# Memory tokens of row tiles 4 to 7 turned on VectorE instead of TensorE, their turns dealt out one by one, and the last sums in banks of their own

## The chip, the core and the metric

The kernel runs on one core of a Trainium2 chip. Its engines work side by side: TensorE (PE in the profile, with its weight loads as a row of their own, PEld), VectorE (DVE), ScalarE (ACT), GpSimd (POOL) and the sync engine (SP), whose queue issues most DMAs. The metric is the device time of one execution in microseconds (us), the median of several.

## What is computed

The reference is a trunk of two layers on 256 tokens of 2048 features, with 256 memory tokens beside them. Cut to what matters here:

```python
for l in range(DEPTH):                      # DEPTH = 2
    h = rmsnorm(x, norm_g[l])
    proj = h @ w_in[l]                      # 2048 -> 7168 columns, three groups of heads
    ...                                     # gated conv, differential attention
    mn = rmsnorm(mem, mem_norm_g[l])
    mkv = mn @ w_mem_kv[l]                  # 2048 -> 1024 columns: keys, values
    ...                                     # attention into the memory tokens
    y = jnp.concatenate([y_a, y_d, y_m], axis=-1) @ w_out[l]
    x = x + y
```

All inputs and the output are float32.

## The kernel before

**Splitting.** Every large product is made of three TensorE passes: each operand is split into a high part (rounded by ScalarE) and a low part (the remainder, taken by VectorE), and hi x hi, lo x hi and hi x lo are summed in PSUM (`products`, L310 to L312, for the input and output projections; the second `products`, L777, for the memory projection).

**The memory stage.** The first 95 us of the program project the memory tokens to keys and values of both layers. The contraction over 2048 features is cut into 16 row tiles of 128; g counts row tiles over both layers, 0 to 31 (`NG`). For every g one tile of weights, 128 rows by 1024 columns (512 KB), is loaded by `weights(g)` into one of four `raw` buffers, and `w_parts(g)` makes its parts: ScalarE multiplies by the norm's gain and rounds (L742), VectorE takes the remainder (L743). Gains of row tiles below `DEALT` come from `cva`, the others from `gm_dealt`. The tokens of row tile k must stand with features on the partitions. `token_parts(k)` splits them into `memT` (L261 on ScalarE, L262 on VectorE), and where they come from depends on `DEALT`, which is 8: below it, `turned(k)` has TensorE transpose two 128x128 blocks of `xs` against an identity (L748). From 8 on, a quarter of the tokens (four row tiles, 512 features) is read by `strips_of` in four DMAs of 128 KB, each to 32 partitions in runs of 512 bytes, and turned by one VectorE transpose of 128x1024 (`strips_turned`, L638); row k of a quarter is then feature 4p + j on partition p. The tokens in natural order are loaded as well for all 16 row tiles (`tokens`), since their squares are summed on ScalarE (`mem_squares`).

**The order.** The stage is written out by hand: `pin` keeps instructions in the order of the program on their engine. Twelve matmuls of 128x512 belong to each g: for each half of the columns two hi x hi (FIRST), then two lo-token x hi-weight and two hi-token x lo-weight (REST), for two halves of tokens. The loop over g (L885) issues FIRST of g, then `operands(g + 2)` (for g = 3 those of 4 and 5), then REST of g, then `beside(g)`, then the second half. `beside(g)` issues on SP's queue, in this order: the natural tokens that `TOKENS` has for g, `weights(g + 4)`, which waits until `w_parts(g)` has freed the buffer, and one small load of constants; then it appends tasks (strips, squares, statistics) that `run_side` carries on, a step for each g. SP issues in order, and the DMA engines serve what it issued in about that order.

Before the loop, SP issues tokens and weights of g = 0 to 3 in the order of L846 to L858, and `operands` of 1 to 3 are made in between.

**The strips of x.** In the same stage the four quarters of x are read as strips and turned (`x_turned`): strips, a pause, one transpose of 128x1024, then two row tiles split in each of two steps. `x_next` uses the same function between the layers.

**The tail.** The last output block (512 columns, second layer) is computed by `block` with `apart=4`: the products of the second half of the tokens (t = 1) for its last four row tiles are left to the end (`late`). Two of them run at full width; the last two run first for columns 0 to 255, then for columns 256 to 511, all in the one PSUM bank `acc[1]`. Then VectorE adds each half to `xs` (L1065) and the halves are stored by DMAs, the first issued by SP, the second by ScalarE's queue (L1068).

Of the kernel before, what the change touches and what calls it, by code (L numbers as in the profile page):

```python
# [11 lines left out]
F32 = mybir.dt.float32  # L12
# [3 lines left out]
ALU = mybir.AluOpType  # L16
# [3 lines left out]
P = 128  # L20
# [19 lines left out]
QT = NB // P  # L40
DEALT = 8

# [7 lines left out]
def encoder(ctx: ExitStack, tc: tile.TileContext, x, mem, norm_g, w_in, conv_w, conv_b,  # L50
# [242 lines left out]
    def block(stat, w, cols, order, steps=1, apart=0, acc=None, more=False,  # L293
# [8 lines left out]
        def ends(k):  # L302
            return k == order[0] and not begun, k == order[-1] and not more
# [14 lines left out]
        for c in range(0, n, CK):  # L318
# [11 lines left out]
            run_side(steps)  # L330
        for t, k, hi, lo in late[:-2]:
            products(acc, t, k, hi, lo, *ends(k))
        for at in range(0, NB, NB // 2):
            half = slice(at, at + NB // 2)
            for t, k, hi, lo in late[-2:]:
                products([a[:, half] for a in acc], t, k, hi[:, half], lo[:, half], False, at > 0 and ends(k)[1])
        return acc

# [296 lines left out]

    def strips_turned(st):
        whole = tmp.tile([P, QT, SEQ], F32, tag="sh", name=nm("xf"))
        pin(nc.vector.transpose(whole.rearrange("p j (n i) -> p j n i", i=B),  # L638
                                st.rearrange("p n (c j) -> p j n c", j=QT)))
        return whole  # L640

    def x_turned(dst, l, q, src, at_once):


        st = yield from strips_of(src, at_once)
        yield 2
        whole = strips_turned(st)
        yield
        for j in range(QT):
            split_T(dst, q * QT + j, whole[:, j], g_norm(l, q * QT + j), pin=True)  # L650
            if j % 2:
                yield

# [96 lines left out]

    dealt = {}

    def mem_turned(q, at_once):
        st = yield from strips_of(mem[:, q * NB:(q + 1) * NB], at_once)
        yield 2
        dealt[q] = strips_turned(st)

# [3 lines left out]

    def operands(g):
        token_parts(g)
        w_parts(g)

# [33 lines left out]

    TOKENS = {0: 4, 1: 6, 8: 8, 9: 10, 10: 12, 11: 14}  # L800
    MEM_STRIPS = {2: 2, 4: 3}
    X_STRIPS = {12: 0, 16: 1, 20: 2, 24: 3}
# [3 lines left out]
    def beside(g):  # L806


        if g + 4 < NG:
            if g in TOKENS:  # L810
                tokens(TOKENS[g], 2)
            weights(g + 4)
        if g in MEM_STRIPS:
            tasks.append(later(mem_turned(MEM_STRIPS[g], 2 if g == 2 else 1), 1))
        if g >= 2:
            for dst, src in islice(constants, 1):
                pin(nc.sync.dma_start(dst, src))
        if g in X_STRIPS:
            q = X_STRIPS[g]
            tasks.append(later(x_turned(xT, 0, q, x[:, q * NB:(q + 1) * NB], 1), 1))  # L820
        if g in (4, 8, 11, 13):
            mem_squares((4, 8, 11, 13).index(g))
        if g == 6:
            distance(1)
        if g == 13:
            tasks.append(later(mem_stats(), 1))
        if g == 21:
            tasks.append(later(rest_of_constants(), 1))
        if g in X_NATURAL:
            x_natural(*X_NATURAL[g])  # L830
        if g in X_SQUARES:
            for t in range(NT):
                x_square(X_SQUARES[g], t)
# [23 lines left out]
    tokens(3, 1)  # L857
    weights(3)  # L858
    warm(6)
    distance(0)  # L860
# [46 lines left out]
    for l in range(DEPTH):  # L907
# [149 lines left out]
        for b in range(4):  # L1057
# [3 lines left out]
            for t in range(NT):  # L1061
                n = 256 if final else NB
                for lo in range(0, NB, n):
                    xc = xs[:, t, b * NB + lo:b * NB + lo + n]
                    nc.vector.tensor_tensor(xc, acc[t][:, lo:lo + n], xc, ALU.add)  # L1065
                    if final:
# [37 lines left out]
```

## Time and profile before

| | us |
|---|---|
| median of 3 runs | 920.17 (920.02 to 920.51) |
| the profiled execution | 919.96 |
| its span, first to last instruction | 918.1 |
| TensorE busy | 913.5 |
| VectorE busy | 675.5 |
| ScalarE busy | 501.9 |
| granted TensorE clock | 0.999 of full |

The span is 1.86 us shorter than the time of the same execution. The profile gives for each engine its busy time, groups of instructions by source line, a timeline of instructions (start, length, engine, line, operation, what it writes and reads, shape, count of merged instructions, and in brackets idle time before it with what ended it), and the transfers of the DMA engines. A letter q behind an engine is its sequencer, which issues DMAs. Lengths of TensorE's records overlap, since matmuls are pipelined; what one costs is the distance from its start to the start of the next.

### The profile page before, as it was taken

The numbers are of one execution on the slowest core, as the hardware profiler recorded it, in microseconds if no ns is written. First come the engines' busy times: TensorE is split into PE (matmuls) and PEld (weight loads), VectorE is DVE, ScalarE is ACT, GpSimd is POOL, SyncE is SP. The second block draws the span as 40 slices with busy tenths as digits, with TensorE's granted clock in tenths as the row PEclk, the third lists the DMA queues.
The fourth block names the chain that finished last, engine by engine and source line by source line (L and its number), as shares of the span: only waits on it lengthen the run. The fifth ranks groups of instructions, "written<-read, shape, count | busy, mean of one in ns | idle before, by whom it ended". The sixth has DMA issues, their size and how long they took to land.

```text
span 918.1 us, 12328 instructions
## 1 busy us (share of the span) xinstructions
PE 913.5 (99%) x4183; PEld 759.4 (83%) x4183; DVE 675.5 (74%) x1197; ACT 501.9 (55%) x770; POOL 7.0 (1%) x18
## 2 busy tenths in 40 slices
PE   9999999999999999999999999999999999999998
PEld 7888888888888888888888888888888888888886
DVE  5889978767898777558676757878898777458652
ACT  6666745675545554446455544568555554446431
POOL 0001000000000000000000000000000000000000
PEclk9999999999999999999999999999999999999999
DMA  9999887875669997989677767885888887978662
GB/s 276 290 286 296 285 256 234 247 215 186 178 221 251 245 258 230 246 259 262 225 256 247 237 199 215 237 232 188 235 231 223 253 234 219 268 243 247 215 220 73
DMA packets 254243, 216.12 MB, mean 235 GB/s; under 512 B 131982, under 2 KB 181476, under 8 KB 254180
## 3 DMA queue, kind: packets, MB, share of 16 engines
q1 hardware_dynamic: 252020, 211.78, 78.4%
q0 software_dynamic: 672, 2.10, 0.7%
q10 hardware_dynamic: 1488, 1.46, 0.5%
q8 instruction: 33, 0.54, 0.2%
q14 instruction: 30, 0.25, 0.1%
HBM read 194.32 MB, written 20.97 MB: 234 GB/s over the span
## 4 chain that ended last, share of the span: by engine, by line
PE 99%; DVE 0%; DVEq 0%; issue 0%
PE acc L310 28%; PE acc L311 28%; PE acc L312 28%; PE acc L777 10%; PE po L447 2%; PE s L555 1%; PE s L554 1%; PE s L607 1%; PE warm L125 0%; PE pt L748 0%; DVE xs L1065 0%; DVEq L1099 0%; PE pva L862 0%; PE pvb L150 0%
## 5 line engine op out<-in xcount | busy, mean ns | idle before, releaser
L290 DVE TENSOR_TENSOR lo<-raw,hi 128x1024 fp32r<-128x1024 f32 x288 | 351.6, 1222 | 179.7 <-ACT hi L289 170.5
L289 ACT CAST hi<-raw 128x1024 fp32r<-128x1024 f32 x288 | 302.5, 1052 | 325.5 <-PE acc L312 254.7
L311 PE MATMUL acc<-lo,xT 128*128 128x512 f32 x896 | 349.0, 390 | 0.0
L312 PE MATMUL acc<-hi,xT 128*128 128x512 f32 x896 | 348.7, 389 | 0.0
L310 PE MATMUL acc<-hi,xT 128*128 128x512 f32 x896 | 348.4, 391 | 0.0
L312 PEld LDWEIGHTS acc<-hi,xT 128*128 128x128 f32 x896 | 168.2, 188 | 35.0
L310 PEld LDWEIGHTS acc<-hi,xT 128*128 128x128 f32 x896 | 168.2, 188 | 33.8
L311 PEld LDWEIGHTS acc<-lo,xT 128*128 128x128 f32 x896 | 168.3, 188 | 33.5
L311 PE MATMUL acc<-lo,yT 128*128 128x512 f32 (+1 forms) x258 | 99.9, 387 | 0.0
L312 PE MATMUL acc<-hi,yT 128*128 128x512 f32 (+1 forms) x258 | 99.9, 387 | 0.0
L310 PE MATMUL acc<-hi,yT 128*128 128x512 f32 (+1 forms) x258 | 99.9, 387 | 0.0
L777 PE MATMUL acc<-hi,memT 128*128 128x512 f32 (+1 forms) x260 | 70.6, 390 | 0.0
L310 PEld LDWEIGHTS acc<-hi,yT 128*128 128x128 f32 x258 | 48.4, 188 | 10.0
L312 PEld LDWEIGHTS acc<-hi,yT 128*128 128x128 f32 x258 | 48.4, 188 | 10.0
L311 PEld LDWEIGHTS acc<-lo,yT 128*128 128x128 f32 x258 | 48.4, 188 | 9.8
L777 PEld LDWEIGHTS acc<-hi,memT 128*128 128x128 f32 x260 | 47.9, 188 | 10.1 <-ACT hi L742 0.5
L777 PE MATMUL acc<-lo,memT 128*128 128x512 f32 (+1 forms) x130 | 39.7, 387 | 0.0
L777 PEld LDWEIGHTS acc<-lo,memT 128*128 128x128 f32 x130 | 24.3, 188 | 5.0
L743 DVE SCALAR_TENSOR_TENSOR lo<-raw,cva,hi 128x1024 fp32r<-128x1024 f32 (+2 forms) x21 | 21.4, 1027 | 6.4 <-ACT hi L742 6.3
L565 ACT ACTIVATE e<-e,mx 128x256 f32<-128x256 f32 x48 | 23.8, 498 | 1.4 <-DVE mx L561 1.3
L743 DVE SCALAR_TENSOR_TENSOR lo<-raw,gm_dealt,hi 128x1024 fp32r<-128x1024 f32 x16 | 20.5, 1279 | 4.7 <-ACT hi L742 3.8
L742 ACT ACTIVATE hi<-raw,cva 128x1024 fp32r<-128x1024 f32 (+2 forms) x21 | 19.7, 947 | 5.6 <-DMA raw<-in_w_mem_kv_dram 5.1
(155 smaller groups left out, 635.3 us busy)
## 6 DMA issues: line engine op xcount, KB each, us to landing
raw<-in_w_in_dram SPq DMA_DIRECT2D x192, 512.0 KB, 4.3
raw<-in_w_out_dram SPq DMA_DIRECT2D x64, 512.0 KB, 4.8
raw<-in_w_in_dram SPq DMA_DIRECT2D x64, 256.0 KB, 4.3
raw<-in_w_mem_kv_dram SPq DMA_DIRECT2D x29, 512.0 KB, 6.3
d<-sh SPq DMA_DIRECT2D x80, 128.0 KB, 3.8
sh<-d SPq DMA_DIRECT2D x64, 128.0 KB, 3.7
d<-yn SPq DMA_DIRECT2D x40, 64.0 KB, 4.5
yn<-d SPq DMA_DIRECT2D x40, 64.0 KB, 3.0
```

The source lines that it names most:

```text
L289: nc.scalar.copy(hi, raw)
L290: nc.vector.tensor_tensor(lo_, raw, hi.bitcast(F32), ALU.subtract)
L310: nc.tensor.matmul(acc[t], sh, hi, start=first, stop=False)
L311: nc.tensor.matmul(acc[t], sh, lo, start=False, stop=False)
L312: nc.tensor.matmul(acc[t], sl, hi, start=False, stop=last)
L447: nc.tensor.matmul(po[:, t, :], eT[:, i, t, k, :], v[:, k, h * P:(h + 1) * P], start=k == 0, stop=k == NT - 1)
L554: nc.tensor.matmul(s[c][:, i, :], qi, k_first(yT, c, h), start=True, stop=False)
L555: nc.tensor.matmul(s[c][:, i, :], qi, k_second(yT, k2, c, h), start=False, stop=True)
L565: nc.scalar.activation(e[:, c, i], e[:, c, i], AF.Exp, bias=mx[:, c, i:i + 1], accum_out=sm[:, c, i:i + 1])
L742: pin(nc.scalar.activation(hi, raw, AF.Copy, scale=gain))
L743: pin(nc.vector.scalar_tensor_tensor(lo, raw, gain, hi.bitcast(F32), ALU.mult, ALU.subtract))
L777: pin(nc.tensor.matmul(accs[l, half][t][:, at:at + n], memT[:, token_part, k, t * P:(t + 1) * P], p, start=k == 0 and at == 0 and token_pa ...
```

## The change

The change has these parts.

- `DEALT` goes from 8 to 4: row tiles 4 to 7 of the memory tokens, too, come from strips, so `turned` is called for four row tiles instead of eight, and their weights take their gains from `gm_dealt`, which has three quarters instead of two.
- The strips of the new quarter (q = 1) are issued before the loop, behind `weights(3)`, and one load of constants behind them; the other constants follow from g = 1 on instead of from g = 2. The strips of q = 2 stay at g = 2, those of q = 3 go from g = 4 (one per step) to g = 5 (two per step).
- The natural tokens of row tiles 4 and 5 are loaded at g = 4 instead of g = 0, those of 6 and 7 at g = 7 instead of g = 1; squares go from g = 4, 8, 11, 13 to 4, 10, 12, 14, the statistics from 13 to 14.
- A quarter's turn is four VectorE transposes of 128x256 (`mem_turn`) instead of one of 128x1024. In `operands(g)` the turn of row tile g + 1 stands between the low part of the tokens and the parts of the weights of g; for g = 4 its own turn and its weights come first.
- For x, a quarter's turn is two transposes of 128x512, the second behind the first two splits.
- In the tail, the two products at full width end the sum in `acc[1]`; each half of the last two products is summed in a PSUM tile of its own (`rest`). VectorE adds `acc[1]` to `xs` at full width first, then each half, and each half is stored as before.

```diff
--- before.py
+++ after.py
@@ -38,7 +38,7 @@
 NA = P // B
 PAIR_EVERY = 9
 QT = NB // P
-DEALT = 8
+DEALT = 4
 
 
 C_X, C_B, C_C, C_G = 0, 768, 1536, 2304
@@ -328,13 +328,16 @@
                     else:
                         products(acc, t, k, hi, lo, *ends(k))
             run_side(steps)
-        for t, k, hi, lo in late[:-2]:
-            products(acc, t, k, hi, lo, *ends(k))
-        for at in range(0, NB, NB // 2):
+        main, tail = late[:-2], late[-2:]
+        for at, (t, k, hi, lo) in enumerate(main):
+            products(acc, t, k, hi, lo, False, at == len(main) - 1)
+        rest = []
+        for at in range(0, NB if tail else 0, NB // 2):
             half = slice(at, at + NB // 2)
-            for t, k, hi, lo in late[-2:]:
-                products([a[:, half] for a in acc], t, k, hi[:, half], lo[:, half], False, at > 0 and ends(k)[1])
-        return acc
+            rest.append(ps_acc.tile([P, NB], F32, tag="acc", name=nm("acc")))
+            for i, (t, k, hi, lo) in enumerate(tail):
+                products({t: rest[-1][:, 0:NB // 2]}, t, k, hi[:, half], lo[:, half], i == 0, i == len(tail) - 1)
+        return acc + rest
 
     def row_stats(ss, tag):
 
@@ -633,23 +636,24 @@
                 yield
         return st
 
-    def strips_turned(st):
-        whole = tmp.tile([P, QT, SEQ], F32, tag="sh", name=nm("xf"))
-        pin(nc.vector.transpose(whole.rearrange("p j (n i) -> p j n i", i=B),
-                                st.rearrange("p n (c j) -> p j n c", j=QT)))
-        return whole
+    def whole_tile():
+        return tmp.tile([P, QT, SEQ], F32, tag="sh", name=nm("xf"))
+
+    def turn_strips(whole, st, at, n):
+        pin(nc.vector.transpose(whole.rearrange("p j (n i) -> p j n i", i=B)[:, at:at + n],
+                                st.rearrange("p n (c j) -> p j n c", j=QT)[:, at:at + n]))
 
     def x_turned(dst, l, q, src, at_once):
 
 
         st = yield from strips_of(src, at_once)
         yield 2
-        whole = strips_turned(st)
-        yield
-        for j in range(QT):
-            split_T(dst, q * QT + j, whole[:, j], g_norm(l, q * QT + j), pin=True)
-            if j % 2:
-                yield
+        whole = whole_tile()
+        for j in range(0, QT, 2):
+            turn_strips(whole, st, j, 2)
+            yield
+            for i in (j, j + 1):
+                split_T(dst, q * QT + i, whole[:, i], g_norm(l, q * QT + i), pin=True)
 
     def x_next(dst, l, q):
 
@@ -748,20 +752,30 @@
             pin(nc.tensor.transpose(pt[:, t * P:(t + 1) * P], xs[:, t, k * P:(k + 1) * P], ident))
         return pt
 
-    dealt = {}
-
-    def mem_turned(q, at_once):
-        st = yield from strips_of(mem[:, q * NB:(q + 1) * NB], at_once)
-        yield 2
-        dealt[q] = strips_turned(st)
+    dealt, strips_in = {}, {}
+
+    def mem_strips(q, at_once):
+        strips_in[q] = yield from strips_of(mem[:, q * NB:(q + 1) * NB], at_once)
+
+    def mem_turn(k):
+        q, j = divmod(k, QT)
+        if j == 0:
+            dealt[q] = whole_tile()
+        turn_strips(dealt[q], strips_in[q], j, 1)
 
     def token_parts(g):
         if g < KT:
             split_T(memT, g, turned(g) if g < DEALT else dealt[g // QT][:, g % QT], None, pin=True)
 
     def operands(g):
+        if g == DEALT:
+            mem_turn(g)
+            w_parts(g)
         token_parts(g)
-        w_parts(g)
+        if DEALT <= g < KT - 1:
+            mem_turn(g + 1)
+        if g != DEALT:
+            w_parts(g)
 
     accs = {}
 
@@ -797,8 +811,8 @@
     def x_natural(c, t):
         pin(nc.sync.dma_start(xs[:, t, c * NB:(c + 1) * NB], x[t * P:(t + 1) * P, c * NB:(c + 1) * NB]))
 
-    TOKENS = {0: 4, 1: 6, 8: 8, 9: 10, 10: 12, 11: 14}
-    MEM_STRIPS = {2: 2, 4: 3}
+    TOKENS = {4: 4, 7: 6, 8: 8, 9: 10, 10: 12, 11: 14}
+    MEM_STRIPS = {2: 2, 5: 3}
     X_STRIPS = {12: 0, 16: 1, 20: 2, 24: 3}
     X_NATURAL = {14: (0, 0), 17: (0, 1), 20: (1, 0), 22: (1, 1), 24: (2, 0), 26: (2, 1), 28: (3, 0), 29: (3, 1)}
     X_SQUARES = {19: 0, 25: 1, 29: 2}
@@ -811,18 +825,18 @@
                 tokens(TOKENS[g], 2)
             weights(g + 4)
         if g in MEM_STRIPS:
-            tasks.append(later(mem_turned(MEM_STRIPS[g], 2 if g == 2 else 1), 1))
-        if g >= 2:
+            tasks.append(later(mem_strips(MEM_STRIPS[g], 2), 1))
+        if g >= 1:
             for dst, src in islice(constants, 1):
                 pin(nc.sync.dma_start(dst, src))
         if g in X_STRIPS:
             q = X_STRIPS[g]
             tasks.append(later(x_turned(xT, 0, q, x[:, q * NB:(q + 1) * NB], 1), 1))
-        if g in (4, 8, 11, 13):
-            mem_squares((4, 8, 11, 13).index(g))
+        if g in (4, 10, 12, 14):
+            mem_squares((4, 10, 12, 14).index(g))
         if g == 6:
             distance(1)
-        if g == 13:
+        if g == 14:
             tasks.append(later(mem_stats(), 1))
         if g == 21:
             tasks.append(later(rest_of_constants(), 1))
@@ -856,6 +870,10 @@
     weights(2, NB, NB)
     tokens(3, 1)
     weights(3)
+    for _ in mem_strips(1, NA):
+        pass
+    for dst, src in islice(constants, 1):
+        pin(nc.sync.dma_start(dst, src))
     warm(6)
     distance(0)
     pv = ps_t.tile([P, NB], F32, tag="t", name="pva")
@@ -1060,9 +1078,14 @@
                         apart=4 if final and b == 3 else 0, acc=accs[b] if b < 2 else None)
             for t in range(NT):
                 n = 256 if final else NB
+                rest = acc[NT:] if t == NT - 1 else []
+                if rest:
+                    xc = xs[:, t, b * NB:(b + 1) * NB]
+                    nc.vector.tensor_tensor(xc, acc[t], xc, ALU.add)
                 for lo in range(0, NB, n):
                     xc = xs[:, t, b * NB + lo:b * NB + lo + n]
-                    nc.vector.tensor_tensor(xc, acc[t][:, lo:lo + n], xc, ALU.add)
+                    part = rest[lo // n][:, 0:n] if rest else acc[t][:, lo:lo + n]
+                    nc.vector.tensor_tensor(xc, part, xc, ALU.add)
                     if final:
                         eng = nc.scalar if lo else nc.sync
                         eng.dma_start(out[t * P:(t + 1) * P, b * NB + lo:b * NB + lo + n], xc)
```

## Prediction

> **What bounds the kernel now.** First the head of the profile's page, then the chain of work that ended last.
>
> ```profile
> span 918.1 us, 12328 instructions
> PE 913.5 (99%) x4183; PEld 759.4 (83%) x4183; DVE 675.5 (74%) x1197; ACT 501.9 (55%) x770; POOL 7.0 (1%) x18
> PE 99%; DVE 0%; DVEq 0%; issue 0%
> ```
>
> TensorE is busy for 913.5 of 918.1 us, and the chain is TensorE from end to end. Busy alone proves little, as records of pipelined matmuls overlap, so I read next the timeline of TensorE in the memory stage (start, length, what, count).
>
> ```profile
> 14.61 0.63 PE L777 MATMUL acc<-hi,memT 128*128 128x512 f32 x2
> 15.08 0.60 PE L748 MATMUL pt<-ident,xs 128*128 128x128 f32 x4
> ...
> 15.97 0.63 PE L777 MATMUL acc<-lo,memT 128*128 128x512 f32 x2
> ...
> 17.81 0.62 PE L777 MATMUL acc<-hi,memT 128*128 128x512 f32 x2
> 18.26 0.38 PE L748 MATMUL pt<-ident,xs 128*128 128x128 f32 x2
> ...
> 18.95 0.63 PE L777 MATMUL acc<-lo,memT 128*128 128x512 f32 x2
> ...
> 20.80 0.62 PE L777 MATMUL acc<-hi,memT 128*128 128x512 f32 x2
> 21.26 0.38 PE L748 MATMUL pt<-ident,xs 128*128 128x128 f32 x2
> ...
> 21.94 0.63 PE L777 MATMUL acc<-lo,memT 128*128 128x512 f32 x2
> ...
> 24.70 0.61 PE L777 MATMUL acc<-lo,memT 128*128 128x512 f32 x2
> ...
> 26.06 0.61 PE L777 MATMUL acc<-lo,memT 128*128 128x512 f32 x2
> ```
>
> From 24.70 to 26.06 lie six matmuls of 128x512 and nothing else: 1.36 us, 0.227 each, so one row tile (twelve) takes 2.72. TensorE waits for nothing there. So the kernel gets shorter only by TensorE work that goes, or behind its last matmul, and longer only where an operand comes too late.
>
> **Part 1: eight transposes leave TensorE.** L748 at 15.08, 18.26 and 21.26 makes the tokens of row tiles 4 and 5, 6, and 7. Between 14.61 and 15.97 stand four matmuls (0.91) and four transposes: 1.36 - 0.91 = 0.45 us. Between 17.81 and 18.95, and between 20.80 and 21.94, four matmuls and two transposes take 1.14 each: 0.23 us twice. Together **0.91 us**, 0.11 for a transpose. The matmuls stay the same in number and shape.
>
> **Part 2: the tail.**
>
> ```profile
> 912.46 0.39 PE L312 MATMUL acc<-hi,yT 128*128 128x512 f32 x1
> ...
> 913.28 0.28 PE L312 MATMUL acc<-hi,yT 128*128 128x256 f32 x1
> ...
> 914.00 0.28 PE L312 MATMUL acc<-hi,yT 128*128 128x256 f32 x1
> 914.32 0.76 DVE L1065 TENSOR_TENSOR xs<-acc,xs 128x256 f32<-128x256 f32 x2 [2.04 <-PE acc L312]
> ```
> ```profile
> L1065 DVE TENSOR_TENSOR xs<-acc,xs x24: 410/416/687, 452.5 to 914.7; 128x256 f32<-128x256 f32 x16, 128x512 f32<-128x512 f32 x8
> ```
>
> Columns 0 to 255 are summed at 913.28 + 0.28 = 913.56, yet their add starts at 914.32 with the other half's, 0.04 behind the last matmul: both adds wait for the bank. Two adds of 0.42 that span 0.76 start 0.34 apart, so the last DMA follows 0.34 later than it must. With banks of their own, the new full-width add (0.69, the maximum of L1065, 128x512) runs from 912.89 to 913.58, the first half's add to about 914.02, and the second starts at 914.32 alone. **0.34 us** go; the new add hides behind the last twelve matmuls (if it came late it would cost up to 0.69).
>
> So far 919.96 - 0.91 - 0.34 = 918.7. What may be late against it is all in the memory stage.
>
> **Part 3: what VectorE takes over at row tile 4.** There is no 128x256 turn in the trace; the nearest rows are these.
>
> ```profile
> L638 DVE STREAM_TRANSPOSE xf<-xt x10: 1981/2020/2033, 24.3 to 520.5; 128x1024 f32<-128x1024 f32 x10
> ```
> ```profile
> L521 DVE STREAM_TRANSPOSE sh<-e 128x512 f32<-128x512 f32 x12 | 8.4, 699 | 0.0
> ```
> ```profile
> 14.15 0.73 ACT L742 ACTIVATE hi<-raw,cva 128x512 fp32r<-128x512 f32 x1
> ```
> ```profile
> 14.91 0.75 DVE L743 SCALAR_TENSOR_TENSOR lo<-raw,cva,hi 128x512 fp32r<-128x512 f32 x1 [0.20 <-ACT hi L742]
> 15.90 0.42 DVE L262 TENSOR_TENSOR memT<-pt,memT 128x256 fp32r<-128x256 f32 x1 [0.23 <-ACT memT L261]
> ```
>
> A quarter of 2.01 us is 0.50; above, the whole of a 128x512 turn, 0.70. I take 0.6. VectorE is free at 14.91 + 0.75 = 15.66: the turn of tile 4 to 16.3, the low part of its weights (1.28, L743 at full width, below) to 17.5, the low part of its tokens (0.42) to 17.9. ScalarE is free at 14.88; its 1.15 for the weights fit, if the weights have landed. TensorE, 0.45 earlier than before, starts tile 4 at 17.36 and wants the low tokens two matmuls later, at 17.8, with a weight load before that:
>
> ```profile
> L777 PEld LDWEIGHTS acc<-hi,memT 128*128 128x128 f32 x260 | 47.9, 188 | 10.1 <-ACT hi L742 0.5
> ```
>
> With its 0.19, some 0.3 us are late at tile 4, from this alone. The turn also adds a wait on VectorE, for the strips; behind it stand both low parts, and TensorE behind them. But the strips lie ahead of the weights in the ring, so the weights come last (part 4). Then VectorE has 0.6 + 0.42 + 1.28 = 2.3 of each 2.72 and catches up. For later quarters four turns of 0.6 replace one of 2.01, which costs VectorE 0.4 but never blocks it for 2 us.
>
> **Part 4: the DMA ring.** This is the term that decides. The windows view gives busy time of each engine, the clock, and last the DMA engines' share and GB/s.
>
> ```profile
> 9.00:15.50 6.50, 6.50 (x34) 5.34 (x33) 4.23 (x7) 3.23 (x7) 0.00 (x0) 1.00 1.02 382
> 15.50:17.00 1.50, 1.50 (x9) 1.25 (x8) 0.64 (x3) 1.50 (x3) 0.00 (x0) 1.00 1.13 211
> 17.00:24.00 7.00, 7.00 (x34) 5.69 (x33) 5.67 (x7) 5.30 (x10) 0.00 (x0) 1.00 1.09 229
> ```
>
> The DMA engines are full throughout (1.02 to 1.13). With weights and natural tokens they move 382 GB/s; from 15.5 on, where the strips of q = 2 and small pieces pass, only 211 and 229. Into this full ring the change puts the strips of q = 1, 512 KB, ahead of the weights of tile 4. At 211 they take 2.5 us, at 382 1.4. Out go, up to tile 8, the natural tokens of two row tiles, 256 KB, 0.7 us at 382 (those of 4 and 5 now stand right before the weights of tile 8). The gain load `gx`, 16 KB, comes one step earlier, also ahead of tile 8: 0.1 at 211.
>
> The Trainium skill, "DMA: Bandwidth & Descriptors", section "Specifications", holds 512 bytes enough for line rate, and the strips' runs are 512 bytes long. By that rule the price would be the 1.4; the windows speak against it, though they mix strips with smaller pieces.
>
> How much delay is free? First tile 8: issue of its weights and their time to landing, then its parts and TensorE.
>
> ```profile
> 18.27 0.35 SPq L735 DMA_DIRECT2D raw<-in_w_mem_kv_dram  x1
> ```
> ```profile
> raw<-in_w_mem_kv_dram SPq DMA_DIRECT2D x1, 512.0 KB, 7.5
> ```
> ```profile
> 26.68 1.15 ACT L742 ACTIVATE hi<-raw,gm_dealt 128x1024 fp32r<-128x1024 f32 x1
> ```
> ```profile
> 27.86 1.28 DVE L743 SCALAR_TENSOR_TENSOR lo<-raw,gm_dealt,hi 128x1024 fp32r<-128x1024 f32 x1 [0.63 <-ACT hi L742]
> ```
> ```profile
> 29.23 1.07 PE L777 MATMUL acc<-hi,memT 128*128 128x512 f32 x4
> 30.14 0.61 PE L777 MATMUL acc<-lo,memT 128*128 128x512 f32 x2
> ```
>
> Landed at 18.27 + 7.5 = 25.8, plus 1.15 and 1.28: ready at 28.2, and read (as lower part) at 30.14. 1.9 us are free; with TensorE 0.91 earlier, **1.0**. Extra ring time ahead of it: 2.5 - 0.7 + 0.1 = **1.9**. So tile 8 is **0.9 us late**. Tile 4, the same way:
>
> ```profile
> 7.37 0.33 SPq L735 DMA_DIRECT2D raw<-in_w_mem_kv_dram  x1
> ```
> ```profile
> raw<-in_w_mem_kv_dram SPq DMA_DIRECT2D x1, 512.0 KB, 6.3
> ```
>
> Its weights landed at 13.7; 2.5 less 0.7 later is 15.5; high part to 16.65, low part to 17.95, low tokens to 18.4 against the 17.8 above: with the weight load some 0.8 late. Tile 7 is a third such place: behind it on VectorE waits the turn of tile 8, which needs the last strip of q = 2. Strips took this long to land:
>
> ```profile
> DMA to landing us min/median/max: 4.7/5.5/6.9
> ```
>
> These lateness terms don't add up: what tile 4 gives back, tile 8 has in hand. The largest counts, **0.9**.
>
> Edits costed at nothing: five more issues on SP ahead of tile 4's weights (0.33 to 0.35 each in the rows above) hide behind a ring that is full until then (cover gone: up to 2 us for that load); fewer natural tokens early and squares later, since nothing on TensorE reads them before the values are emptied at g = 17; the halved turns of x, since TensorE never waited for x.
>
> **Sum.** 919.96 - 0.91 - 0.34 + 0.9 = 919.6. The profiled execution lies 0.21 below the median of the three runs, so against the median this is **919.8**. About 0.2%, 1.84 us, is what a measurement can tell from no change; "faster" means below 918.3, "slower" above 922.0.
>
> **The rivals.**
>
> *Forecast: the gain is mostly given back where weights land late.* 919.2 to 920.8, 45%. For it: the full ring. Against: 1.0 us of free time is close to the 1.9.
>
> *The strips are hidden.* If they pass at 382 GB/s, the extra is 0.8, under the 1.0 free, and only the 0.3 at tile 4 remains: 919.0, or 918.7 without it; by the median 918.9 to 919.2. 28%. The page's rule on 512 bytes leads here.
>
> *The strips clog the ring, and the kernel is slower.* From 15.5 to 24.0 the ring moved 1.5 x 211 + 7 x 229 = 1920 KB, which at 382 take 5.0 us; it took 8.5. If the 3.5 lost are the price of about one quarter's strips, the new quarter costs 1.4 + 3.5 = 4.9, the extra ahead of tile 8 is 4.3 and the delay 3.3: 919.96 - 1.25 + 3.3 = 922.0, by the median 922.2. It is slower than before from an extra of 2.3 on, by over 0.2% from 4.1 on. For it: tile 8's weights took 7.5 us against 6.3 for tile 4's. Against: small pieces share the blame. 19%, of which 8 lie above 922.0.
>
> *The tail's halves still wait for the last matmul*, because something else ties them: 0.34 more, 920.1. 4%.
>
> *A removed transpose frees its whole record.*
>
> ```profile
> L748 PE MATMUL pt<-ident,xs x16: 270/272/475, 3.7 to 21.4; 128*128 128x128 f32 x16
> ```
>
> Eight of 0.272 are 2.18: 919.96 - 2.18 - 0.34 = 917.4 with nothing late. Against it stand the distances of part 1, 0.11 each: the records overlap. 4%. The Trainium skill, "TensorE: Matmul & The Clock Gate", section "Part 4: PE-mode transpose", gives about 275 ns for one in a kernel (in bf16); the record agrees, the distance does not.
>
> **How the numbers follow.** Faster by over 0.2% only in the last rival: 4%. Slower: 8%. The rest, 88%, is no change. The range runs from 918.6 (everything hidden) to 921.5, which leaves out the top of the clogged ring and the last rival.
>
> **What would show it.** No L748 behind tile 3, and starts of L777 there 0.227 apart. The tail: three adds on VectorE, the last starting alone some 0.3 behind the start of the last matmul. Late operands: TensorE's idle ended by L743 or L262 at tiles 4, 7 and 8, and weights of tile 8 that land at about 27.7 (18.27 + 7.5 + 1.9). Wrong would make it a ring that passes the strips at 382 GB/s, or a VectorE that falls behind over several tiles.

## The result and the profile after

| | before | after |
|---|---|---|
| median of 6 runs, us | 920.18 (919.95 to 920.51) | 925.21 (923.38 to 925.94) |
| the profiled execution | 919.96 | 925.07 |
| its span | 918.1 | 923.3 |
| start of the last matmul | 914.00 | 919.29 |

The ratio is 1.0052, with a 95% interval of 1.0041 to 1.0062: the kernel is 5.0 us slower, and the time lies outside the range of the prediction. First the head, the chain and one costly group of the page of after.

```profile
span 923.3 us, 12339 instructions
PE 916.9 (99%) x4175; PEld 757.5 (82%) x4175; DVE 679.8 (74%) x1216; ACT 502.4 (54%) x770; POOL 7.0 (1%) x18
...
PE 91%; DMA 5%; DVE 3%; ACT 1%; issue 1%; SPq 0%; ACTq 0%; DVEq 0%
...
L746 ACT ACTIVATE hi<-raw,gm_dealt 128x1024 fp32r<-128x1024 f32 x24 | 27.5, 1149 | 13.3 <-DMA raw<-in_w_mem_kv_dram 13.3
```

Eight matmul records fewer (4183 to 4175) are the transposes. The chain was TensorE from end to end before; now 9% of it are loads of weights and the engines behind them. The high parts of the weights (L746, formerly L742) waited 13.3 us for their load. Next the waits from 4 to 102 us (waiter, releaser, sum, times, longest), after and then before.

```profile
ACT hi L746 <- DMA raw<-in_w_mem_kv_dram: 17.6, 19, 2.1
...
PEld acc L791 <- DVE lo L747: 3.7, 8, 0.7
...
PEld acc L791 <- ACT hi L746: 1.1, 3, 0.6
PEld acc L791 <- DVE memT L262: 1.1, 1, 1.1
```
```profile
ACT hi L742 <- DMA raw<-in_w_mem_kv_dram: 8.0, 9, 1.8
...
PEld acc L777 <- ACT hi L742: 0.5, 1, 0.5
```

Loads of weights are late twice as long. Before, TensorE's weight loads (PEld) waited once for parts of weights, 0.5 us; now they wait for them eleven times (L747, L746) and once for tokens (L262, 1.1 us). The timeline of TensorE shows three of the places: tile 4, the second layer, and the end of the stage.

```profile
18.90 0.73 PE L791 MATMUL acc<-hi,memT 128*128 128x512 f32 x2 [0.63 <-DVE memT L262]
...
82.55 0.73 PE L791 MATMUL acc<-lo,memT 128*128 128x512 f32 x2 [0.32 <-DVE lo L747]
...
99.56 0.50 PE L310 MATMUL acc<-hi,xT 128*128 128x512 f32 x1 [0.38 <-ACT kraw L800]
```
```profile
94.94 0.39 PE L310 MATMUL acc<-hi,xT 128*128 128x512 f32 x1
```

The second fence is before: the projections begin at 94.94 there and at 99.56 after. So 4.6 us are lost by the end of the memory stage. Where starts of matmuls lie further apart than the 0.227 of their neighbours, the excess after is 1.2 us at tile 4, 0.8 at tiles 10 and 11, 0.75 at 52 to 56 us, 0.6 at 82 and 1.9 from 93 to 101: lateness comes again and again. Last the windows (before, then after): DMA share and GB/s are the last two columns.

```profile
9.50:15.00 5.50, 5.50 (x28) 4.47 (x27) 3.23 (x7) 2.73 (x6) 0.00 (x0) 1.00 1.03 384
15.00:35.00 20.00, 20.00 (x94) 16.46 (x92) 15.24 (x18) 14.01 (x25) 0.00 (x0) 1.00 1.05 274
...
45.00:75.00 30.00, 30.00 (x134) 24.52 (x133) 25.53 (x57) 21.13 (x36) 0.00 (x0) 1.00 0.99 277
...
95.00:100.00 5.00, 5.00 (x24) 4.14 (x23) 4.78 (x8) 5.00 (x11) 0.00 (x0) 1.00 0.68 232
```
```profile
9.50:15.00 5.50, 5.50 (x27) 4.45 (x27) 3.28 (x7) 2.71 (x5) 0.00 (x0) 1.00 1.12 247
15.00:35.00 20.00, 19.36 (x83) 14.71 (x82) 15.07 (x22) 11.67 (x19) 0.00 (x0) 1.00 1.08 261
...
45.00:75.00 30.00, 29.93 (x129) 23.70 (x128) 24.43 (x55) 21.19 (x35) 0.00 (x0) 1.00 1.05 276
...
95.00:100.00 5.00, 4.49 (x19) 3.09 (x18) 4.34 (x6) 3.76 (x6) 0.00 (x0) 1.00 1.04 378
```

The ring is fuller after and moves less for it. GB/s divided by share, called the quotient from here on, compares bytes with the time that their packets take; it is no rate of the ring, as shares above 1 show. It falls from 261 to 242 at 15 to 35 us, and from 280 to 263 at 45 to 75 us, where the first layer's additions have landed. Before, the ring is idle at times near the end of the stage (0.68); after, it is full to the end.

### The profile page after: what moved, and what is told of

Its sections match the earlier page's. It is cut to its first block, busy times and chain, and to the rows that moved or that the text cites. A ratio compares the mean times of both kernels' runs of the same rounds, so it can differ in the third digit from the quotient of the medians.

```text
span 923.3 us, 12339 instructions
## 1 busy us (share of the span) xinstructions
PE 916.9 (99%) x4175; PEld 757.5 (82%) x4175; DVE 679.8 (74%) x1216; ACT 502.4 (54%) x770; POOL 7.0 (1%) x18
## 4 chain that ended last, share of the span: by engine, by line
PE 91%; DMA 5%; DVE 3%; ACT 1%; issue 1%; SPq 0%; ACTq 0%; DVEq 0%
PE acc L311 28%; PE acc L312 28%; PE acc L310 28%; DMA raw<-in_w_mem_kv_dram 5%; PE acc L791 2%; PE po L450 2%; DVE lo L747 1%; ACT hi L746 1%; PE s L558 1%; PE s L557 1%; PE s L610 1%; DVE xf L643 0%; DVE xT L265 0%; DVE lo L290 0%; ACT mv L806 0%
## 5 line engine op out<-in xcount | busy, mean ns | idle before, releaser
L747 DVE SCALAR_TENSOR_TENSOR lo<-raw,gm_dealt,hi 128x1024 fp32r<-128x1024 f32 x24 | 30.6, 1274 | 6.9 <-ACT hi L746 6.6
L746 ACT ACTIVATE hi<-raw,gm_dealt 128x1024 fp32r<-128x1024 f32 x24 | 27.5, 1149 | 13.3 <-DMA raw<-in_w_mem_kv_dram 13.3
L643 DVE STREAM_TRANSPOSE xf<-xt 128x512 f32<-128x512 f32 (+1 forms) x28 | 25.1, 897 | 1.3 <-DMA vb<-in_conv_b_dram 1.3
```

Of the source, the lines that this page charges most:

```text
L746: pin(nc.scalar.activation(hi, raw, AF.Copy, scale=gain))
L747: pin(nc.vector.scalar_tensor_tensor(lo, raw, gain, hi.bitcast(F32), ALU.mult, ALU.subtract))
```

## The experiments

Eighteen kernels ran. "Before plus" or "the change with" says which kernel was edited; a time is a median, a ratio is to the kernel before on the same chip.

**The parts that cost no load (e1).** Before plus the new tail and the halved turns of x.

> The kernel before with two parts of the change only: the tail's halves in banks of their own, and the turns of x in halves. If the loss comes from the memory tokens alone (their DMAs or their turns on VectorE), this is 0.1 to 0.35 us faster than before, about 919.9 to 920.1, and TensorE waits nowhere in the memory stage. If the halved turns of x cost TensorE time at 50 to 100 us, where the changed kernel shows waits, this is 1 us or more slower than before.

920.09, ratio 0.9998 (0.9988 to 1.0007): no loss here, and no gain that can be told from nothing. For the tail, the timeline of the change itself:

```profile
918.18 0.69 DVE L1084 TENSOR_TENSOR xs<-acc,xs 128x512 f32<-128x512 f32 x1 [0.60 <-PE acc L312]
...
918.98 0.42 DVE L1088 TENSOR_TENSOR xs<-acc,xs 128x256 f32<-128x256 f32 x1
...
919.29 0.28 PE L312 MATMUL acc<-hi,yT 128*128 128x256 f32 x1
919.61 0.42 DVE L1088 TENSOR_TENSOR xs<-acc,xs 128x256 f32<-128x256 f32 x1 [0.21 <-PE acc L312]
```

The last half's add starts 0.32 behind the last matmul's start and is over at 920.03, 0.74 behind it; before, the pair ended at 914.32 + 0.76, 1.08 behind. That is the predicted 0.34. But the span ends 4.0 us behind that matmul against 4.1 before (923.3 - 919.29, 918.1 - 914.00): some 0.1 arrives.

**The added load alone (e2, e3).** Before plus 512 KB behind `weights(3)` that nobody reads.

```diff
     weights(3)
+    for _ in strips_of(mem[:, NB:2 * NB], NA):
+        pass
```

> The kernel before, and beside it the four strip loads of quarter 1 (512 KB, 512-byte runs into 32 partitions each) issued right behind the weights of tile 3, as the change has them; nothing reads them, all else is as before, the eight transposes included. If the strips in the full DMA ring make the weights land late, this is 3 to 6 us slower than before, with waits of TensorE from tile 4 on. If the loss comes from the order on VectorE or from the dealt turns, the weights have up to 1.9 us in hand and this is within 1 us of before.

922.35, ratio 1.0023 (1.0014 to 1.0033). In e3 the same bytes go to 128 partitions in runs of 1 KB.

> The kernel before with the same 512 KB in the same place in the same number of DMAs, but in another form: each of the four writes all 128 partitions in runs of 1 KB (natural order); nothing reads them. If the bytes alone decide, it is as slow as the run with the strips. If the form decides (short runs into 32 partitions), the ring takes them at some 380 GB/s in 1.4 us, under the 1.9 us that the weights of tile 8 have in hand, and this is within 1 us of before.

922.17, ratio 1.0021 (1.0011 to 1.0030). The added loads cost about 2 us in either form, less than the 3 to 6 and more than the 1 of the two expectations. Bytes and number of loads are the same in both, so these runs don't tell which of the two costs. The form shows in the ring (e2, then e3) but not at the end:

```profile
9.50:15.00 5.50, 5.50 (x28) 4.46 (x27) 3.23 (x7) 2.71 (x6) 0.00 (x0) 1.00 1.12 289
```
```profile
9.50:15.00 5.50, 5.50 (x28) 4.46 (x26) 3.25 (x6) 2.73 (x6) 0.00 (x0) 1.00 1.06 378
```

**The gain alone (e5, e13).** Before without the eight transposes; row tiles 4 to 7 take other tokens.

```diff
-            split_T(memT, g, turned(g) if g < DEALT else dealt[g // QT][:, g % QT], None, pin=True)
+            split_T(memT, g, xs[:, 0, 0:SEQ] if 4 <= g < DEALT else turned(g) if g < DEALT else dealt[g // QT][:, g % QT], None, pin=True)
```

> The kernel before without the eight transposes of row tiles 4 to 7: their parts are made from natural tokens that lie in SBUF, so these four tiles are not turned at all, and no DMA is added. By the sum of the prediction TensorE saves 0.91 us: 919.3 against 920.2. If the late operands at tile 4 came from VectorE alone, nothing of it would show here, as no turn is added; if a removed transpose freed its whole record of 272 ns, it would be 918.0.

920.15, ratio 0.9994 (0.9983 to 1.0004): nothing arrives. VectorE and, behind it, TensorE at tile 12:

```profile
36.12 1.98 DVE L638 STREAM_TRANSPOSE xf<-xt 128x1024 f32<-128x1024 f32 x1
38.57 0.43 DVE L262 TENSOR_TENSOR memT<-xf,memT 128x256 fp32r<-128x256 f32 x1 [0.47 <-ACT memT L261]
39.63 1.28 DVE L743 SCALAR_TENSOR_TENSOR lo<-raw,gm_dealt,hi 128x1024 fp32r<-128x1024 f32 x1 [0.63 <-ACT hi L742]
```
```profile
39.65 1.20 PE L777 MATMUL acc<-hi,memT 128*128 128x512 f32 x4
40.97 0.73 PE L777 MATMUL acc<-lo,memT 128*128 128x512 f32 x2
```

Tokens and weights of tile 12 stand behind the 1.98 of the quarter's turn; the low weights are ready at 39.63 + 1.28 = 40.91, and TensorE starts with them at 40.97. In e13 the turns of quarters 2 and 3 are dealt out one row tile at a time as well, in the order of the change, with all loads as before.

> The run without the eight transposes and without any added load (920.15, which gained nothing, with TensorE waiting 0.8 us around 40 us, tile 12), and now with the turns of quarters 2 and 3 dealt out in the order of the change; quarters 2 and 3 and all DMAs as before, row tiles 4 to 7 still not turned. If the whole 2 us turn on VectorE at tile 12 takes back what the transposes saved, this is 919.2 to 919.4. If something else in the stage is bound within 0.9 us of TensorE, it stays at 920.

919.27, ratio 0.9987 (0.9977 to 0.9996): 0.9 us under the 920.18 above, 1.2 by the ratio, and no such wait. By the interval the gain is 0.4 to 2.1 us. So the transposes are worth about what was predicted, if the quarter's turn is cut up.

**Loads and order in the change (e4, e6, e8, e9, e12).** e4 brings the natural tokens of row tiles 4 to 7 behind all others (g = 12, 13), their squares and the statistics to g = 15.

> The changed kernel with the natural tokens of row tiles 4 to 7 loaded at g = 12 and 13 instead of 4 and 7, their squares at g = 15 and the statistics from 15 on; nothing else differs. Theory one: the natural tokens that stand on SP's queue right ahead of the weights of tiles 8 and 11 make these late while the DMA ring is full. Then this gets back 2 us or more of the 5: 923 or less. Theory two: the ring is short of time in the whole memory stage, and only the total of bytes counts. Then moving 512 KB within the stage changes little: 924 to 926.

927.62, ratio 1.0067 (1.0042 to 1.0092). Neither expectation held, since a new wait came in: TensorE waited 1.94 us for the values to be emptied, and ScalarE, which empties them, had waited 1.95 us for the statistics (`stm`), which come later here:

```profile
57.35 2.22 PE L791 MATMUL acc<-hi,memT 128*128 128x512 f32 x4 [1.94 <-ACT mv L806]
```

e6 loads them at g = 0 and 1 as before.

> The changed kernel with the natural tokens of row tiles 4 to 7 loaded at g = 0 and 1, as before the change; the strips of quarter 1 stay ahead of the weights of tile 4. Its order of DMAs up to tile 8 is then that of the run that added only the strips (922.35). Theory one (the moved tokens stand ahead of the wrong weights): about 922, with TensorE late at tile 4 by another 1 us but not from 8 on. Theory two (the bytes in the stage): 924 to 926.

925.01, ratio 1.0044 (1.0029 to 1.0058). No better: at tile 4 alone some 1.7 us are lost. e8 has the strips of q = 3 one per step from g = 4.

> The changed kernel with the strips of quarter 3 as before the change: from g = 4, one DMA for each step, instead of two for each of two steps from g = 5. If the pairs of strips at g = 5 and 6 hold up the weights of tiles 10 to 12 behind them on SP's queue, this gets back 1 to 2 us: 923.5 to 924. If not, 925 as the changed kernel.

923.5, ratio 1.0031 (1.0017 to 1.0045): 1.7 us under the change, as expected, though the two intervals overlap. e9 puts the next turn behind the weights:

```diff
         token_parts(g)
+        w_parts(g)
         if DEALT <= g < KT - 1:
             mem_turn(g + 1)
```

> The changed kernel with another order on VectorE and ScalarE: for every row tile tokens, then weights, then the turn of the next row tile, tile 4 included (there its own turn comes first); all DMAs as in the change. The wait at tile 4 (TensorE waited for the low part of the tokens, which stood behind the low part of the weights) shrinks from 1.2 to some 0.4 us. If the order on VectorE carries the loss, 923.5 or less; if the landing of the weights does, the 0.8 are given back later and this is 925, as the changed kernel.

931.14, ratio 1.0110 (1.0084 to 1.0137). VectorE in that kernel:

```profile
18.59 0.63 DVE L643 STREAM_TRANSPOSE xf<-xt 128x256 f32<-128x256 f32 x1
...
20.74 1.28 DVE L747 SCALAR_TENSOR_TENSOR lo<-raw,gm_dealt,hi 128x1024 fp32r<-128x1024 f32 x1 [0.63 <-ACT hi L746]
21.95 0.63 DVE L643 STREAM_TRANSPOSE xf<-xt 128x256 f32<-128x256 f32 x1
```

From turn to turn 3.36 us pass instead of 2.72: turn, cast of tokens and high weights on ScalarE, low weights and the next turn on VectorE form a closed loop. The order of the change is needed. e12 gives tile 4 the order of the other tiles.

> The changed kernel with row tile 4 in the order of all others: its own turn, its tokens, the turn of tile 5, its weights (the change has its weights ahead of its tokens). The wait at tile 4, 1.2 us, becomes 0.3 to 0.6. If what tile 4 loses is given back by what comes behind (the waits do not add up), this is 924.5 to 925.5, no better than the change. If they add up, 924.3 or less.

924.81, ratio 1.0046 (1.0031 to 1.0061): the order of tile 4 is not what costs the 5 us.

**The change without loads (e10, e11).** e10 fills the tile of q = 1 by GpSimd instead of loading it; e11 leaves out the natural tokens of row tiles 4 to 7 (512 KB; their squares are taken elsewhere).

> The changed kernel without the four strip loads of quarter 1: the strips' tile is filled with a constant by GpSimd, so row tiles 4 to 7 are not the tokens; all turns, splits, matmuls and the other DMAs stay. Bytes from HBM are those of before. Theory ring (the added load makes weights late): the 5 us go, 919 to 920. Theory order (the dealt turns and the moved loads cost VectorE and SP time by themselves): 923 or more. Between the two, each has its part.

> The changed kernel without the natural tokens of row tiles 4 to 7 (512 KB less, so the bytes of before), the squares of quarter 1 taken from quarter 0; the strips of quarter 1 stay ahead of the weights of tile 4. If the sum of bytes in the memory stage decides, this is about as fast as the run without the strips' load; if the place ahead of the weights of tile 4 decides, it stays near 925. By the ring's count the weights of tiles 8 to 12 have 0.7 to 1.4 us less ahead of them: I expect 921 to 922.5.

e10: 924.98, ratio 1.0049 (1.0031 to 1.0067). e11: 921.8, ratio 1.0013 (1.0003 to 1.0024). e10 has no byte more than before (but for 2 KB of gains a layer) and loses as much as the change. The added load cannot be the one cause. Nor does the sum of bytes decide: e11 has the same bytes as e10 and loses 3 us less.

**Moved loads on a clean base (e18, e19), and the rest without them (e14, e17).** e18 and e19 are e13 with one move each.

> Base is e13 (919.27): tokens 4 to 7 are not turned at all (their operands come from other data), quarters 2 and 3 turned one row tile at a time, no load added. Here only the natural tokens of row tiles 4 to 7 move from g = 0 and 1 to g = 4 and 7, right ahead of the weights of tiles 8 and 11 on SP, and the squares and sums of squares that read them come later, as in the change. Theory (a moved load ahead of weights costs time by itself, because the weights behind it are issued late): weights of tiles 8 and 11 issued 2 to 4 us later than before, TensorE waits at tiles 8 to 11, 921 to 923. Rival (only the added bytes and the turns cost; moving bytes costs nothing): 919.3.

> Base is e13 (919.27), with tokens 4 to 7 not turned. Here only the strips of q = 3 move: two at g = 5 and two at g = 6 in place of one each from g = 4 to 7. Theory (the change lost 1.7 us by this, 925.2 against 923.5 of e8): weights of tiles 9 to 11 are issued later; on a ring without the added load half of it is left, 919.8 to 921. Rival (it costs only when the ring is already behind): 919.3.

e18: 920.0, ratio 0.9995 (0.9985 to 1.0005); e19: 919.32, ratio 0.9988 (0.9979 to 0.9998). Against e13, e18 loses 0.7, which the intervals don't tell from nothing, and e19 nothing; the losses that their theories gave did not come. e14 is the change with loads at their old places.

> The change with all its moved loads at the places of before: natural tokens of row tiles 4 to 7 at g = 0 and 1, squares and their sum at the old steps, strips of q = 3 one by one from g = 4. Left of the change are the added 512 KB of strips of q = 1, the turns on VectorE one by one, the order at tile 4, and the tail. Theory (moved loads cost about half, the added bytes about 2 to 3 us, the tail and the transposes give 1.2 back): 921 to 922.5. Rival (the added load alone is enough, the moves only change where it is paid): 924.5 to 925.5, as the change itself.

923.12, ratio 1.0031 (1.0018 to 1.0044): between the two expectations. And the whole computation with the tail and the dealt turns, but transposes of row tiles 4 to 7 left on TensorE:

> Computes all of the reference. The kernel before, its loads and its transposes of row tiles 0 to 7 on TensorE, with the change's tail, the halved turns of x, and the turns of quarters 2 and 3 one row tile at a time. Theory (the turns one by one take away the wait behind the 2-us turn at tile 12, which is hidden here while TensorE has 0.91 us more to do; the tail gives 0.1 to 0.3): 919.6 to 920.0, and no wait in the memory stage. Rival (the dealt turns cost VectorE 0.4 us a quarter more and it falls behind): above 920.5.

919.66, ratio 0.9992 (0.9982 to 1.0001): 0.7 us by the ratio, which the interval doesn't tell from nothing.

**What is left (e20, e21).** e20 is e14 without the added load, e21 is e10 without the turns of row tiles 4 to 7 and the order at tile 4.

> The change without the load of the strips of q = 1 (as in e10: GpSimd fills the tile that VectorE turns, so row tiles 4 to 7 get other tokens) and with all moved loads back at the places of before (as in e14). Left are the tail, the eight transposes gone, the turns on VectorE and the order at tile 4. Theory (VectorE's turns and the order fit as long as no load is late; lateness needs added bytes or moved loads): about 919.0 to 919.6, no wait beyond 0.5 us at tile 4. Rival (VectorE's part itself is the cause): 921 or more with waits ended by VectorE.

> The change without the load of the strips of q = 1, without the turns of row tiles 4 to 7 on VectorE (their operands come straight from other data) and without the special order at tile 4; both moves of loads stay (tokens of 4 to 7 at g = 4 and 7, strips of q = 3 in pairs from g = 5). Theory (moved loads cost what they do in e10 only because VectorE's turns make weight buffers free later): 919.3 to 920.5. Rival (the two moves together are the cause without VectorE, the ring being full): 923 to 925, as e10, with weights of tile 10 landing at about 34.

e20: 922.43, ratio 1.0021 (1.0009 to 1.0033). e21: 924.18, ratio 1.0043 (1.0028 to 1.0058). Both went the rival's way in time: with neither added load nor moves e20 loses 3 us against e13, and VectorE's turns are not what costs e21 its 4 us against e18, since it has none. What both have, and e13, e17, e18 and e19 have not, are constants one step earlier, a larger table of gains, and something that nothing so far has spoken of. `DEALT` is also read in `weights` (L731 of before):

```python
        if k < DEALT:
            rows = w_mem_kv[l][k * P:(k + 1) * P]
        else:
            rows = x_row_tiles(w_mem_kv[l], k - k % CK)[:, k % CK]
```

With tokens from strips, row tile 4q + j holds every fourth feature, so its weights are every fourth row: 128 rows of 4 KB at a pitch of 16 KB, instead of one block of 512 KB. The change does that to row tiles 4 to 7 in both layers. How the kernels differ with the three is seen with the weights of tile 7 (issue on SP, high part on ScalarE), in e18 as a block, then in e21 as every fourth row; the strips of q = 2 pass at the same time in both.

```profile
15.67 0.35 SPq L742 DMA_DIRECT2D raw<-in_w_mem_kv_dram  x1
```
```profile
20.50 1.15 ACT L749 ACTIVATE hi<-raw,cva 128x1024 fp32r<-128x1024 f32 x1
```
```profile
16.10 0.35 SPq L739 DMA_DIRECT2D raw<-in_w_mem_kv_dram  x1
```
```profile
23.56 1.15 ACT L746 ACTIVATE hi<-raw,gm_dealt 128x1024 fp32r<-128x1024 f32 x1 [1.81 <-DMA raw<-in_w_mem_kv_dram]
```

At most 4.8 us from issue to use, against 7.5 with ScalarE waiting. The rows are not the only difference here: the load of `gx` (16 KB) is issued at 13.48 in e21, ahead of these weights, and at 18.56 in e18, behind them. The windows of the two, e18 and then e21:

```profile
9.50:24.00 14.50, 14.50 (x67) 11.92 (x67) 10.84 (x17) 9.79 (x19) 0.00 (x0) 1.00 0.90 266
...
45.00:75.00 30.00, 30.00 (x133) 24.56 (x132) 26.38 (x63) 21.79 (x39) 0.00 (x0) 1.00 1.01 285
```
```profile
9.50:24.00 14.50, 14.50 (x67) 11.90 (x66) 9.46 (x14) 9.12 (x18) 0.00 (x0) 1.00 0.98 224
...
45.00:75.00 30.00, 29.25 (x124) 22.57 (x123) 24.51 (x55) 21.82 (x36) 0.00 (x0) 1.00 1.05 276
```

The quotient is 296 against 229, and in the second layer 282 against 263. The same quotient from the windows of all kernels:

| `DEALT`, and with it the weights of row tiles 4 to 7 | kernels | 15 to 35 us | 45 to 75 us |
|---|---|---|---|
| 8, a block | before, e1, e2, e3, e5, e13, e17, e18, e19 | 260 to 281 | 267 to 291 |
| 4, every fourth row | after, e4, e6, e8 to e12, e14, e20, e21 | 203 to 259 | 242 to 269 |

The two groups all but part: the low end of one touches the high end of the other. e2 and e3 are late, too, and stay in the first group (281 and 261; 276 and 267), so lateness alone doesn't put a kernel into the second.

Are the rows the reason? Before reads row tiles 8 to 15 of each layer that way, so it can be asked. Three of its windows, with what SP issued in or just ahead of them: at 35 to 40 us such rows (tiles 13 to 15) and natural tokens, no strips; at 50 to 60 blocks (g = 20 to 23, issued from 48.46 to 57.18) beside strips of x; at 60 to 70 such rows (g = 24 to 27, issued from 60.13 to 67.82) beside strips of x.

```profile
35.00:40.00 5.00, 5.00 (x24) 4.14 (x23) 3.90 (x4) 2.50 (x4) 0.00 (x0) 1.00 0.89 330
50.00:60.00 10.00, 10.00 (x46) 8.29 (x45) 6.32 (x5) 6.11 (x9) 0.00 (x0) 1.00 1.07 298
60.00:70.00 10.00, 10.00 (x44) 7.96 (x44) 9.76 (x21) 6.67 (x11) 0.00 (x0) 1.00 1.03 291
```

The quotients are 371, 279 and 283: beside strips of x, rows at this pitch do no worse than blocks. And e11, whose weights of g = 24 are issued at 59.57 and which reads the same rows beside the same strips at that time, comes to 271 and 235:

```profile
60.00:65.00 5.00, 5.00 (x24) 4.14 (x23) 4.89 (x12) 4.18 (x8) 0.00 (x0) 1.00 1.06 287
65.00:70.00 5.00, 5.00 (x23) 3.85 (x22) 4.83 (x14) 3.04 (x4) 0.00 (x0) 1.00 1.07 251
```

So e11, with `DEALT` = 4, has the lower quotient even where both kernels read the same rows, and without lateness: no two matmul starts lie over 0.12 us further apart than usual in these windows of e11. The rows of tiles 4 to 7 may have a part in the loss, but they are not shown to be its cause.

What the runs do show is that the three things together cost some 3 us (e20 against e13; e20 also has VectorE's turns) to 4 us (e21 against e18; e21 also has the pairs of strips, which cost nothing in e19). Which of the rows, the constants one step earlier and the larger table of gains does it, and how, stays open; no kernel changed one of them alone. From e13, this costs 3.2 us in e20; the moves on top of it 2.5 (e10), not the 0.7 they cost without it; the added load on top 0.7 (e14) or 0.2 (after against e10), not the 2.2 of e2. By the intervals each of these differences is uncertain by 1.4 to 2 us, so the last two can't be told from nothing, and the shares depend on the order of counting.

## Why the prediction was wrong

- **Part 1, transposes, 0.91: right** in size. e13 has it; e5 shows that it arrives only with the turn at tile 12 cut up.
- **Part 2, the tail, 0.34: right on VectorE**, the size at the end is some 0.1.
- **Part 3, VectorE at tile 4: not seen by itself.** The turn took 0.63 for the 0.6 assumed, but e10, with the turns and the order of the change and without its added load, starts tile 4's matmuls without a gap over 0.1 us, where 0.3 was expected from VectorE alone. With the added load TensorE lost 1.2 us there instead of 0.8.
- **"The largest counts, 0.9": this step failed.** It took every lateness as given back by the next place and looked at none behind tile 8. Tile 8 came as forecast: its weights were there at 28.1 or just before (their high part started at 28.16 on that load), 0.4 behind the 27.7, and TensorE lost some 0.2 there. But 0.8 more went at tiles 10 and 11 and 3.25 in the second layer. The ring stays full (shares of 0.97 to 1.12 from 9.5 us to the end of the stage) and gave nothing back, and the places of lateness add up to 5.3 us.
- **Part 4, the ring: its price failed, too.** "Extra ring time ahead of it: 2.5 - 0.7 + 0.1 = 1.9" counts only bytes that are added, taken out or moved earlier, at the rates of before. e20 has neither the added load nor the moves, and is still 3.2 us above e13. What else hangs on `DEALT`, but for `gx`, was put at nothing; which part of it costs the time stays open. The window with 211 GB/s was rightly put down to strips and small pieces: tile 8's weights, the first in every fourth row, are issued at 18.27, behind it; in the one with 229 they have a place.
- **"Fewer natural tokens early", costed at nothing: wrong.** What reads them was weighed, not what stands beside them on SP. Before, they passed at g = 0 and 1; after, their issue waits until an earlier load of weights has landed, and the weights behind them on the queue wait with it. Issues of natural tokens from 4 to 50 us, after and then before (waiter, releaser, sum, times, longest):

```profile
SPq L729 <- DMA raw<-in_w_mem_kv_dram: 4.4, 4, 1.4
```
```profile
SPq L725 <- DMA raw<-in_w_mem_kv_dram: 0.9, 1, 0.9
```

  The timeline of SP after:

```profile
19.64 0.40 SPq L729 DMA_DIRECT2D xs<-in_mem_dram  x1
20.14 0.41 SPq L739 DMA_DIRECT2D raw<-in_w_mem_kv_dram  x1
...
30.35 0.39 SPq L729 DMA_DIRECT2D xs<-in_mem_dram  x1
30.84 0.41 SPq L739 DMA_DIRECT2D raw<-in_w_mem_kv_dram  x1
```

  Tile 8's weights are issued at 20.14 (18.27 before) and tile 11's at 30.84 (26.16 before). What such an issue waits for is in the trace's semaphores: in before and after, SP's loads share eight of them in turn, and from 8 us on none is issued until the load eight issues earlier has landed. The tokens at 30.35 stand eight issues behind the weights of 22.23, which landed at 30.33; the weights of 34.03 stand eight behind those of 25.81, which landed at 33.96. So a load of half a KB holds one of eight places as one of 512 KB does, and a count of bytes misses it. The "five more issues on SP", costed by the 0.33 to 0.35 us of an issue, have the same fault. How much of the 5 us goes this way was not tested.
- **The rival of the clogged ring, 922.2, was the nearest.** That e2 measured 922.35 does not confirm its price: e2 keeps the transposes, the old tail and the early tokens, and the rival's 4.9 less the 1.9 free would have put it at 920.2 + 3.0 = 923.2. It put the loss at tile 8, where TensorE lost some 0.2.
- **The rule on 512 bytes** (the Trainium skill, "DMA: Bandwidth & Descriptors", "Specifications"): the quotient is 258 with 512-byte runs in e2 and 357 with 1-KB runs in e3, so here 512 bytes over 32 partitions were not enough, though the time was the same.

## What to carry to other kernels

When a change turns a constant, follow every place that reads it, and ask of each load not only how many bytes it has but when it is issued, which earlier load its issue waits for, and what stands behind it. Where a ring stays full, don't take lateness as paid once: a load that moves can cost everything queued behind it, so compare GB/s and share over the whole stage. A gain on the bounding engine arrives only if the next engine has as much in hand: cut up its longest block first.

## What the hardware showed that was not expected

- **The same rows at different rates.** Loads of rows at a pitch of 16 KB give quotients of 371 without strips and 283 beside strips of x (before), and of 271 and 235 in e11 beside the same strips. The pitch alone does not set the rate; what else does is open.
- **The clock.** In e4, around the 1.94 us of idle time above, the granted clock (third column from the end) fell:

```profile
50.00:55.00 5.00, 4.12 (x17) 2.89 (x16) 3.36 (x10) 4.66 (x10) 0.00 (x0) 1.00 1.10 290
55.00:60.00 5.00, 2.98 (x8) 1.89 (x7) 2.45 (x9) 2.70 (x4) 0.00 (x0) 0.80 1.06 289
60.00:65.00 5.00, 5.00 (x20) 4.08 (x20) 4.96 (x9) 4.04 (x8) 0.00 (x0) 0.86 1.05 265
```

  TensorE was busy 4.12 and 2.98 us of two times five. The four matmuls from 57.35 to 59.37 took 0.51 us each for the usual 0.227, so part of the loss of e4 is matmuls at a lower clock, up to 65 us.
- **Spread.** Two kernels whose loads are late vary more than the kernel before beside them: 923.38 to 925.94 after against 919.95 to 920.51 in six runs each, and 920.73 to 925.07 in e20 (10 runs) against 919.51 to 922.02 (13 runs).
